# V projections of two head groups: 512 columns at once, weights in quarters of 256 rows

## Chip, cores and metric

The kernel runs on one core of a Trainium2 chip. The metric is the device time of one execution in microseconds (us). A core has TensorE (matmuls), VectorE, ScalarE, GpSimd and SyncE; the profile calls them PE, DVE, ACT, POOL and SP, and PEld is TensorE's weight load. Each engine runs its instructions in the order in which they were written out, and waits at semaphores for the others. Matmuls write to PSUM; GpSimd works on SBUF only.

## What is computed

Two layers of a trunk with 512 tokens and a width of 1024. In each, the normalised input `h` (512 x 1024) goes through one input projection, whose columns belong to three groups of heads: a (differential attention), b (stick-breaking), c (forgetting). Each group has q, k, v and gate columns, 512 of each:

```
h = rms_norm(x, g_pre)
p = h @ w_in
qa, ka, va, ga, qs, ks, vs, gs, qf, kf, vf, gf, ff = split(p)
ya = merge(diff_attention(rope(qa), rope(ka), va)) * silu(ga)
yb = merge(stick_breaking_attention(qs, ks, vs)) * silu(gs)
yc = merge(forgetting_attention(qf, kf, vf, cumsum(log_sigmoid(ff)))) * silu(gf)
x = x + rms_norm(concat([ya, yb, yc]) @ w_out, g_post)
```

All of it is in float32.

## The kernel before

A float32 product is made of three matmuls in the fp32r format. Each operand is kept as a rounded high part and the low rest, and `mm3` (L191) adds high x high, high x low and low x high in PSUM: L192, L193 and L194. The normalised input lies in SBUF, transposed, as two such parts (`hT`, 8 chunks of 128 rows by 512 tokens).

A weight unit has 256 columns of `w_in` and comes in two halves of 512 rows. `load_to` fetches a half into one of three `raw` buffers (SP's queue, L167). `split_to` makes the two parts of it in one of four `whl` buffers: ScalarE copies the high part in one instruction (L176, 128x1024), GpSimd subtracts it to get the low part in four pieces of 128x256 (L182). `load_to(st_split[0] + 3)` after each split asks for the raw tile three halves on.

Two forms of projection use the units. `proj_T` (q, k, gates) has the weights as the stationary operand and `hT` as the moving one, 512 columns wide, 24 matmuls for 128 output columns. `proj_N` (V) has a 128-token block of `hT` stationary and the weights moving, 256 columns wide: 24 matmuls for 128 tokens by 256 columns. ScalarE copies the result to the `v` tile (L649).

The order is written out by hand. `do(cost, fn)` puts a piece of projection on a planned time line (`now`, in planned ns) and moves it on by `cost`; `at(t, fn)` puts a side step at a planned time. In the end all steps are sorted by time and written out, so that the plan sets each engine's order, not its times. `use(k, t)` notes when half k is first needed, and its split is written out `lead` ns ahead of that.

For every layer the groups are projected in the order a, c, b: first V (8 blocks of `proj_N`, first unit's four token blocks, then the second's), then q, k, q, k (8 `proj_T`). While a group is projected, the attention of the group before it is run as side steps: `step_a` during c's projection, `step_c` during b's, `step_b` during the gates'. A score tile (L339) goes to VectorE, which adds the mask and takes the minimum (L364); then come exponentials on ScalarE (L373), transposes (L347) and the product with V.

After a projection of q or k, `qk_done` lets ScalarE copy the high part (L319) and VectorE make the low one (L324); for group a, VectorE's rope comes first (L303 to L307):

```
d = 2000 if roped else 0
return (rope_stages(st, scale) if roped else []) + [(d, hi), (d + 796, lo)]
```

Those numbers are plan times after the projection's end. The attention steps of a begin at 3518 after the start of c's stretch, those of c at 3191 after the start of b's.

Of the kernel before, what the change touches and what calls it, by code (L numbers as in the profile page):

```python
# [10 lines left out]
F32 = mybir.dt.float32  # L11
F32R = mybir.dt.float32r
BF16 = mybir.dt.bfloat16
AF = mybir.ActivationFunctionType
# [3 lines left out]
S = 512  # L18
DEPTH = 2
KC = D // 128  # L20
NT = S // 128
# [39 lines left out]
def hybrid_kernel(ctx, tc, x, w_in, forget_bias, diff_lambda, diff_subln, w_out, pre_norm, post_norm, consts, out):  # L61
    nc = tc.nc
# [5 lines left out]
    whl_p = P("whl", 4)  # L68
# [11 lines left out]
    pj_p = P("pj", 3, space=PS)  # L80
# [51 lines left out]
    now = [0.0]  # L132

    def do(cost, fn):
        main.append((now[0], 1, len(main), fn))
        now[0] += cost

    def at(t, fn):
        side.append((t, 0, len(side), fn))


    halves = []
# [3 lines left out]
    def add_in_unit(l, c0, extra=None):  # L146
        w = UW + (8 if extra is not None else 0)
        k0 = len(halves)
        for h in range(2):
            rows = w_in[l, h * 512:(h + 1) * 512]  # L150
            src = [(rows[:, c0:c0 + UW].rearrange("(k p) c -> p k c", p=128), 0, UW)]
            if extra is not None:
                src.append((rows[:, extra:extra + 8].rearrange("(k p) c -> p k c", p=128), UW, w))
            halves.append(dict(src=src, shape=[4, w], pool=whl_p, tag="whl", lead=9500 if h == 0 else 8000))
        return k0

    def add_out_unit(l, kc0, half, pool, tag):
        src = w_out[l, kc0 * 128:(kc0 + 2) * 128, half * S:(half + 1) * S].rearrange("(k p) c -> p k c", p=128)
        halves.append(dict(src=[(src, 0, S)], shape=[2, S], pool=pool, tag=tag, lead=10833))
        return len(halves) - 1  # L160
# [30 lines left out]
    def mm3(ps, lh, ll, rh, rl, first, last):  # L191
        nc.tensor.matmul(out=ps, lhsT=lh, rhs=rh, start=first, stop=False)  # L192
        nc.tensor.matmul(out=ps, lhsT=lh, rhs=rl, start=False, stop=False)  # L193
        nc.tensor.matmul(out=ps, lhsT=ll, rhs=rh, start=False, stop=last)  # L194
# [18 lines left out]
    def proj_N(k0, w, tt, hT, done):  # L213

        st = {}
        sl = slice(tt * 128, (tt + 1) * 128)

        def go(q):
            if q == 0:
                st["ps"] = pj_p.tile([128, w], F32, name="pj", tag="pj")  # L220
            for kc in range(4 * q, 4 * q + 4):
                u = halves[k0 + kc // 4]["hl"][:, :, kc % 4, :]
                h = hT()
                mm3(st["ps"], h[0][:, kc, sl], h[1][:, kc, sl], u[:, 0], u[:, 1], kc == 0, kc == KC - 1)

        for q in range(2):
            do(1290, lambda q=q: go(q))
        for t, fn in done(st):
            at(now[0] + t, fn)


    def pre_norm_stages(st, tt, hT):
# [307 lines left out]
    def decay_sum(lf, l):  # L540
        pt = pt_p.tile([8, S], F32, name="pt", tag="pt")
        for t in range(NT):
            nc.tensor.transpose(out=pt[:, t * 128:(t + 1) * 128], in_=lf[:, t * 8:(t + 1) * 8], identity=C["ident"])
        cum = cb_p.tile([8, S], F32, name="cum", tag="cb")
        nc.vector.tensor_tensor_scan(out=cum, data0=pt, data1=C["chunk"][0:8], initial=0.0, op0=ALU.add, op1=ALU.bypass)
        nc.sync.dma_start(out=cs[l], in_=cum)
# [6 lines left out]
    def steps(fn, c, t0, span, w=W_STEP):  # L553
        t = t0
        for p in range(4):
            for i in range(NT):
                fn(t, c, p, i)
                t += span / 16 * w[i]
# [3 lines left out]
    def use(k, t):  # L562
        uses.append((k, t))
# [43 lines left out]
    def plan_layer(l, L):  # L607
        hT = L["hT"]
# [8 lines left out]
        for g in ("a", "c", "b"):  # L617
            base = G[g]
            c = dict(pairs=[{} for _ in range(4)], lc=lc)
            st = {}  # L620
            c["v"] = lambda st=st: st["v"]
            c["o"] = lambda st=st: st["o"]
            c["cs"] = cs[l]
            t0 = now[0]
            at(t0, lambda st=st: st.update(v=v_p.tile([128, NT, 512], F32, name="v", tag="v")))
            if prev is not None:
                pst, pc, pg = prev
                at(t0, lambda pst=pst: pst.update(o=o_p.tile([128, 4, S], F32, name="o" + pg, tag="o")))
                steps(step_a if pg == "a" else step_c, pc, t0 + (3518 if pg == "a" else 3191), 50075 if pg == "a" else 46774)
            order = [(u, tt) for u in range(2) for tt in range(NT)]  # L630
            if g == "a":
                order = [(0, 0), (0, 1), (0, 2), (1, 0), (1, 1), (1, 2), (0, 3), (1, 3)]
            ks = []
            for u in range(2):
                ks.append(add_in_unit(l, base + 1024 + u * UW, 6144 if g == "a" and u == 0 else None))
            seen = set()
            for u, tt in order:
                ex = g == "a" and u == 0
                w = UW + (8 if ex else 0)
                if u not in seen:  # L640
                    seen.add(u)
                    use(ks[u], now[0])
                    use(ks[u] + 1, now[0] + 1300)
                    if g == "a" and u == 1:
                        halves[ks[u]]["lead"], halves[ks[u] + 1]["lead"] = 7500, 6500

                def done(pst, u=u, tt=tt, ex=ex, st=st, w=w):
                    def ev():
                        nc.scalar.activation(out=st["v"][:, tt, u * UW:(u + 1) * UW], in_=pst["ps"][:, 0:UW],  # L649
                                             func=AF.Copy)  # L650
                        if ex:
                            if "ff" not in ffd:
                                ffd["ff"] = lay.tile([128, 32], F32, name="ff", tag="ff")
                            nc.vector.tensor_copy(ffd["ff"][:, tt * 8:(tt + 1) * 8], pst["ps"][:, UW:w])
                    return [(0, ev)]
                proj_N(ks[u], w, tt, hT, done)
            if g == "a":
                at(now[0] + 2000, lambda: layer_consts(lcd, l))
                at(now[0] + 5000, lambda: ffd.update(lf=decay(ffd["ff"], lcd, l)))
                at(now[0] + 9000, lambda: decay_sum(ffd["lf"], l))  # L660
            sc = 0.125 if g == "b" else -0.125
            for u in range(2):
                for part in ("q", "k"):
                    k0 = add_in_unit(l, base + u * UW + (512 if part == "k" else 0))
                    use(k0, now[0])
                    use(k0 + 1, now[0] + 2600)
                    if g == "a" and u == 0 and part == "q":
                        for h in range(2):
                            halves[k0 + h].update(lead=2500, lo="both")
                    for cc in range(2):  # L670
                        keep = c["pairs"][2 * u + cc]
                        if part == "q":
                            proj_T(k0, cc, hT, lambda pst, keep=keep: qk_done(pst, g == "a", sc, keep, "q"))
                        else:
                            proj_T(k0, cc, hT, lambda pst, keep=keep: qk_done(pst, g == "a", 1.0, keep, "k"))
            prev = (st, c, g)
            ctxs[g] = (st, c)
# [27 lines left out]
        for g in ("b", "a", "c"):  # L705
            ost = ctxs[g][0]
            for u in range(2):
                k0 = add_in_unit(l, G[g] + 1536 + u * UW)
# [24 lines left out]
        order = [("a", 0), ("a", 2), ("c", 0), ("c", 2), ("b", 0), ("b", 2)]  # L733
        acc = {}
        for u, (g, j0) in enumerate(order):
            k = add_out_unit(l, row[g] + j0, 0, whl_p, "whl")
            use(k, now[0])
            for jj in range(2):
                for tt in range(NT) if (u, jj) == (5, 1) else (3, 0, 1, 2):
                    def go(u=u, g=g, j=j0 + jj, jj=jj, tt=tt, k=k):  # L740
                        if u == 0 and jj == 0:
                            acc[tt] = (pj_p if tt < 3 else s_p).tile([128, S], F32, name="acc",
                                                                    tag="pj" if tt < 3 else "s")
                        y, w = ys[g, j], halves[k]["hl"]
                        sl = slice(tt * 128, (tt + 1) * 128)
                        mm3(acc[tt], y[:, 0, sl], y[:, 1, sl], w[:, 0, jj], w[:, 1, jj],
                            u == 0 and jj == 0, u == 5 and jj == 1)
# [29 lines left out]
        for u, (g, j0) in enumerate(order):  # L777
            k = add_out_unit(l, row[g] + j0, 1, *((o_p, "o") if u < 3 else (v_p, "v") if u == 3 else (whl_p, "whl")))
# [3 lines left out]
        for tt in range(NT):  # L782
            sl = slice(tt * 128, (tt + 1) * 128)
            st = {}
# [56 lines left out]
    for l in range(DEPTH):  # L841
        L = plan_layer(l, L)
# [38 lines left out]
```

## Time and profile before

| | |
|---|---|
| time, median of 3 runs | 873.25 us (873.04 to 873.48) |
| time of the profiled execution | 873.66 us |
| its span, first to last instruction | 871.8 us |
| instructions | 13938 |
| TensorE busy | 854.9 us, 98% of the span |
| VectorE / ScalarE / GpSimd busy | 495.3 / 476.9 / 449.6 us |

The profile is one execution. A row of a timeline is a start, a length, the engine, the line in the kernel, the operation, output<-input with shapes, a count, and in brackets how long the engine sat idle before it and what ended the wait. Matmuls are pipelined, so that a matmul's length is longer than the distance to the next start; that distance, the pitch, is what one costs in a row of them.

### The profile page before, as it was taken

How to read it: one execution, taken by the hardware profiler on the slowest of the kernel's cores; microseconds unless marked ns; L12 is line 12 of the kernel's file. 1: busy time of each engine (PE TensorE's matmuls, PEld its weight loads, DVE VectorE, ACT ScalarE, POOL GpSimd, SP SyncE). 2: the span in 40 equal slices, each digit the busy share in tenths (PEclk: the TensorE clock that was granted, in tenths of full speed). 3: DMA queues.
4: the chain of work that ended last, by engine and by line, in shares of the span. 5: the costliest groups of instructions: out<-in, count | busy, mean ns of one | idle time of the engine just before them, and what ended most of it. 6: DMA issues, size and time to landing. Idle time of an engine off the chain costs nothing.

```text
span 871.8 us, 13938 instructions
## 1 busy us (share of the span) xinstructions
PE 854.9 (98%) x4892; PEld 721.4 (83%) x4892; DVE 495.3 (57%) x1143; ACT 476.9 (55%) x1064; POOL 449.6 (52%) x680
## 2 busy tenths in 40 slices
PE   7999999999999999999999999999999999999997
PEld 5988998898778778777898889888987787877885
DVE  5378656544565778623563875664445476774322
ACT  4344667766776556633334356676667756664310
POOL 4366554655444548770364664555554544688301
PEclk9999999999999999999999999999999999999999
DMA  7365323432524221237264452325335422122522
GB/s 233 89 164 138 96 73 98 117 102 76 154 67 116 75 72 49 73 107 257 78 177 114 123 145 74 99 72 146 97 81 137 106 66 72 49 78 92 164 101 97
DMA packets 73207, 94.27 MB, mean 108 GB/s; under 512 B 6433, under 2 KB 56225, under 8 KB 73138
## 3 DMA queue, kind: packets, MB, share of 16 engines
q1 hardware_dynamic: 70834, 89.19, 35.6%
q10 hardware_dynamic: 2304, 4.20, 1.5%
q8 instruction: 39, 0.64, 0.3%
q14 instruction: 30, 0.25, 0.1%
HBM read 76.56 MB, written 4.23 MB: 93 GB/s over the span
## 4 chain that ended last, share of the span: by engine, by line
PE 78%; DVE 10%; ACT 4%; POOL 3%; issue 2%; DMA 2%; DVEq 0%; POOLq 0%; ACTq 0%; SPq 0%
PE pj L192 18%; PE pj L194 18%; PE pj L193 17%; PE s L339 6%; PE pt L347 5%; PE ov L437 4%; POOL hl L182 2%; PE acc L192 2%; PE acc L193 2%; PE acc L194 2%; PE ov L399 2%; DVE ra L307 2%; DVE sh L306 2%; DVE sh L303 1%; DVE qd L324 1%
## 5 line engine op out<-in xcount | busy, mean ns | idle before, releaser
L182 POOL TENSOR_TENSOR hl<-raw,hl 128x256 fp32r<-128x256 f32 (+1 forms) x420 | 343.5, 850 | 237.1 <-ACT hl L176 213.0
L192 PE MATMUL pj<-hT,hl 128*128 128x512 f32 x576 | 236.6, 411 | 0.0
L194 PE MATMUL pj<-hT,hl 128*128 128x512 f32 x576 | 225.7, 392 | 0.0
L193 PE MATMUL pj<-hT,hl 128*128 128x512 f32 x576 | 225.3, 391 | 0.0
L176 ACT ACTIVATE hl<-raw 128x1024 fp32r<-128x1024 f32 (+1 forms) x120 | 126.3, 1058 | 35.4 <-DMA raw<-in_w_out_dram 18.9
L194 PEld LDWEIGHTS pj<-hT,hl 128*128 128x128 f32 x576 | 108.1, 188 | 24.3
L192 PEld LDWEIGHTS pj<-hT,hl 128*128 128x128 f32 x576 | 108.4, 188 | 20.0 <-issue 2.1
L193 PEld LDWEIGHTS pj<-hT,hl 128*128 128x128 f32 x576 | 108.7, 189 | 16.9
L192 PE MATMUL pj<-hl,hT 128*128 128x256 f32 (+1 forms) x384 | 112.2, 292 | 0.3 <-ACT hT L257 0.2
L194 PE MATMUL pj<-hl,hT 128*128 128x256 f32 (+1 forms) x384 | 109.5, 285 | 0.5 <-DVE hT L258 0.5
L193 PE MATMUL pj<-hl,hT 128*128 128x256 f32 (+1 forms) x384 | 109.3, 285 | 0.5 <-POOL hl L182 0.5
L373 ACT ACTIVATE p<-p,mn 128x128 f32<-128x128 f32 (+3 forms) x128 | 71.1, 556 | 33.6 <-DVE mn L364 31.7
L506 DVE TENSOR_TENSOR_SCAN kp<-kp,c_masks 128x128 f32<-128x128 f32 (+3 forms) x64 | 67.2, 1051 | 18.3 <-ACT kp L499 17.8
L192 PEld LDWEIGHTS pj<-hl,hT 128*128 128x128 f32 x384 | 73.7, 192 | 1.3 <-ACT hT L257 1.0
L193 PEld LDWEIGHTS pj<-hl,hT 128*128 128x128 f32 x384 | 73.8, 192 | 1.2 <-POOL hl L182 0.7
L194 PEld LDWEIGHTS pj<-hl,hT 128*128 128x128 f32 x384 | 73.5, 191 | 1.2 <-DVE hT L258 1.2
L339 PE MATMUL s<-kd,qd 128*128 128x128 f32 (+1 forms) x192 | 62.6, 330 | 2.9 <-DVE mn L364 2.9
L350 ACT ACTIVATE pT<-pt 128x128 f32<-128x128 f32 (+3 forms) x96 | 41.2, 443 | 37.5 <-PE pt L347 37.2
L339 PE MATMUL s<-kd,qs 128*128 128x128 f32 (+1 forms) x192 | 61.2, 323 | 0.0
L511 DVE TENSOR_TENSOR sg<-sg,kp 128x127 f32<-128x127 f32 (+3 forms) x64 | 46.1, 721 | 5.5
L185 DVE TENSOR_TENSOR hl<-raw,hl 128x1024 fp32r<-128x1024 f32 (+2 forms) x18 | 21.0, 1175 | 44.8 <-ACT hl L176 44.7
L466 ACT ACTIVATE p<-p,rc 128x128 f32<-128x128 f32 (+3 forms) x64 | 35.0, 556 | 20.2 <-DVE rc L464 20.2
(142 smaller groups left out, 1453.0 us busy)
## 6 DMA issues: line engine op xcount, KB each, us to landing
raw<-in_w_in_dram SPq DMA_DIRECT2D x96, 512.0 KB, 3.7
qs<-qd SPq DMA_DIRECT2D x48, 256.0 KB, 4.5
raw<-in_w_out_dram SPq DMA_DIRECT2D x24, 512.0 KB, 3.6
cb<-cs ACTq DMA_DIRECT2D x16, 256.0 KB, 3.3
xl<-in_x_dram SPq DMA_DIRECT2D x4, 512.0 KB, 4.9
xt<-in_x_dram SPq DMA_DIRECT2D x8, 256.0 KB, 6.1
xs<-xt SPq DMA_DIRECT2D x8, 256.0 KB, 2.0
xt<-xs SPq DMA_DIRECT2D x8, 256.0 KB, 3.9
```

The lines of the kernel that those rows point to most:

```text
L176: nc.scalar.activation(out=hl[:, 0], in_=raw, func=AF.Copy)
L182: nc.gpsimd.tensor_tensor(out=hl[:, 1, k, c:e], in0=raw[:, k, c:e], in1=hl[:, 0, k, c:e].bitcast(F32), op=ALU.subtract)
L192: nc.tensor.matmul(out=ps, lhsT=lh, rhs=rh, start=first, stop=False)
L193: nc.tensor.matmul(out=ps, lhsT=lh, rhs=rl, start=False, stop=False)
L194: nc.tensor.matmul(out=ps, lhsT=ll, rhs=rh, start=False, stop=last)
L339: nc.tensor.matmul(out=s[:, 0:n], lhsT=pr[q][:, m, i * 128:n], rhs=pr["k"][:, m, 0:n], start=(j == 0), stop=(j == 1))
L347: nc.tensor.transpose(out=pt[:, j * 128:(j + 1) * 128], in_=p[:, j * 128:(j + 1) * 128], identity=C["ident"])
L350: nc.scalar.activation(out=t, in_=src, func=AF.Copy)
L373: nc.scalar.activation(out=p[:, 0:n], in_=p[:, 0:n], func=AF.Exp, bias=st["mn", m], scale=-1.0, accum_out=su)
L466: nc.scalar.activation(out=p[:, 0:n], in_=p[:, 0:n], func=AF.Copy, scale=r)
L506: nc.vector.tensor_tensor_scan(out=rv, data0=rv, data1=C["first"][:, S - n:S][:, ::-1], initial=0.0, op0=ALU.mult, op1=ALU.max)
L511: nc.vector.tensor_tensor(out=sg[:, 0:n - 1], in0=sg[:, 0:n - 1], in1=kp[:, 1:n], op=ALU.mult)
```

## The change

Groups b and c no longer use `add_in_unit` and `proj_N` for V, but `add_v_unit` and `proj_V`: four quarters of 256 rows by 512 columns, each in one `whl` buffer, and four token blocks of 24 matmuls with 512 moving columns. Each quarter is still split by one copy on ScalarE and four pieces on GpSimd, two for each 128 rows. The quarters' leads are 9500, 8000, 5100 and 3800, and the two halves of the first q unit behind them get leads of 3800 and 5100. Group a is as it was.

```diff
+    def add_v_unit(l, c0):
+
+        k0 = len(halves)
+        for h in range(4):
+            src = w_in[l, h * 256:(h + 1) * 256, c0:c0 + S].rearrange("(k p) c -> p k c", p=128)
+            halves.append(dict(src=[(src, 0, S)], shape=[2, S], pool=whl_p, tag="whl", lead=(9500, 8000, 5100, 3800)[h]))
+        return k0
...
+    def proj_V(k0, tt, hT, done):
+
+        st = {}
+        sl = slice(tt * 128, (tt + 1) * 128)
+
+        def go(q):
+            if q == 0:
+                st["ps"] = pj_p.tile([128, S], F32, name="pj", tag="pj")
+            h = hT()
+            for kc in range(2 * q, 2 * q + 2):
+                u = halves[k0 + q]["hl"][:, :, kc % 2]
+                mm3(st["ps"], h[0][:, kc, sl], h[1][:, kc, sl], u[:, 0], u[:, 1], kc == 0, kc == KC - 1)
+
+        for q in range(4):
+            do(1296, lambda q=q: go(q))
+        at(now[0], lambda: done(st["ps"]))
...
-            for u in range(2):
+            if g != "a":
+                order = []
+                kv = add_v_unit(l, base + 1024)
+                for h in range(4):
+                    use(kv + h, now[0] + 1296 * h)
+                for tt in range(NT):
+                    proj_V(kv, tt, hT, lambda ps, st=st, tt=tt: nc.scalar.activation(out=st["v"][:, tt], in_=ps, func=AF.Copy))
+            for u in range(2 if g == "a" else 0):
                 ks.append(add_in_unit(l, base + 1024 + u * UW, 6144 if g == "a" and u == 0 else None))
...
+                    if g != "a" and u == 0 and part == "q":
+                        for h in range(2):
+                            halves[k0 + h]["lead"] = (3800, 5100)[h]
```

## Rows read from the trace of the kernel before

**Rows 1.** The page, part 1: busy us, share of the span, count

```profile
PE 854.9 (98%) x4892; PEld 721.4 (83%) x4892; DVE 495.3 (57%) x1143; ACT 476.9 (55%) x1064; POOL 449.6 (52%) x680
```

**Rows 2.** Waits of TensorE: total us, times, longest; the largest group

```profile
PE s L339 <- DVE mn L364: 2.9, 4, 1.1
```

**Rows 3.** Stretches of the V projections, layer 0: length, busy us per engine

```profile
84.35:115.90 31.55, 30.37 (x249) 29.79 (x248) 17.98 (x57) 20.34 (x53) 16.23 (x24) 1.00 0.33 91
178.18:208.76 30.58, 30.58 (x254) 29.89 (x253) 12.39 (x61) 20.69 (x53) 17.63 (x31) 1.00 0.28 83
```

**Rows 4.** Timeline, TensorE: first and last of 36 matmuls of 256 columns

```profile
25.02 0.28 PE L192 MATMUL pj<-hl,hT 128*128 128x256 f32 x1
...
29.21 0.28 PE L194 MATMUL pj<-hl,hT 128*128 128x256 f32 x1
```

**Rows 5.** Timeline, TensorE: first and last of 149 matmuls of 512 columns

```profile
50.55 0.39 PE L193 MATMUL pj<-hT,hl 128*128 128x512 f32 x1
...
84.13 0.39 PE L194 MATMUL pj<-hT,hl 128*128 128x512 f32 x1
```

**Rows 6.** Timeline, ScalarE, start of group c, layer 0

```profile
85.18 1.28 ACT L319 ACTIVATE kd<-ra 64x512 fp32r<-64x512 f32 x2 [3.24 <-DVE ra L307]
86.49 1.06 ACT L176 ACTIVATE hl<-raw 128x1024 fp32r<-128x1024 f32 x1
90.78 1.28 ACT L319 ACTIVATE kd<-ra 64x512 fp32r<-64x512 f32 x2 [3.23 <-DVE ra L307]
```

**Rows 7.** Timeline, VectorE, the same stretch

```profile
88.55 1.05 DVE L306 SCALAR_TENSOR_TENSOR sh<-sh,rope 128x512 f32<-128x512 f32 x1
89.64 1.11 DVE L307 TENSOR_TENSOR ra<-ra,sh 128x512 f32<-128x512 f32 x1
91.45 1.40 DVE L324 SCALAR_TENSOR_TENSOR kd<-ra,kd 64x512 fp32r<-64x512 f32 x2 [0.70 <-ACT kd L319]
```

**Rows 8.** Timeline, GpSimd: four split pieces merged, then the second and third singly

```profile
87.62 3.72 POOL L182 TENSOR_TENSOR hl<-raw,hl 128x256 fp32r<-128x256 f32 x4 [1.89 <-ACT hl L176]
...
88.32 0.74 POOL L182 TENSOR_TENSOR hl<-raw,hl 128x256 fp32r<-128x256 f32 x1
...
89.01 1.19 POOL L182 TENSOR_TENSOR hl<-raw,hl 128x256 fp32r<-128x256 f32 x1
```

**Rows 9.** Timeline, TensorE: a score and the matmul behind it; the longest wait

```profile
88.67 0.22 PE L339 MATMUL s<-kd,qd 128*128 128x128 f32 x1
...
88.84 0.33 PE L192 MATMUL pj<-hl,hT 128*128 128x256 f32 x1
...
93.24 0.39 PE L339 MATMUL s<-kd,qd 128*128 128x256 f32 x1 [1.09 <-DVE mn L364]
```

**Rows 10.** Timeline, start of the kernel: two split pieces, a matmul released by them

```profile
11.06 2.44 POOL L182 TENSOR_TENSOR hl<-raw,hl 128x264 fp32r<-128x264 f32 x2 [1.31 <-ACT hl L176]
...
13.55 0.39 PE L193 MATMUL pj<-hl,hT 128*128 128x264 f32 x1 [0.51 <-POOL hl L182]
```

**Rows 11.** Timeline, ScalarE and GpSimd, start of group b, layer 0

```profile
178.38 1.20 ACT L319 ACTIVATE kd<-pj 64x512 fp32r<-64x512 f32 x2 [1.86 <-PE pj L194]
179.60 1.06 ACT L176 ACTIVATE hl<-raw 128x1024 fp32r<-128x1024 f32 x1
...
180.74 2.83 POOL L182 TENSOR_TENSOR hl<-raw,hl 128x256 fp32r<-128x256 f32 x4 [4.66 <-ACT hl L176]
```

**Rows 12.** Timeline, TensorE and ScalarE, end of c's stretch, layer 0

```profile
108.55 0.22 PE L339 MATMUL s<-kd,qd 128*128 128x128 f32 x1
...
115.90 0.48 PE L192 MATMUL pj<-hT,hl 128*128 128x512 f32 x1
...
110.28 0.60 ACT L350 ACTIVATE wT<-pt 128x512 f32<-128x512 f32 x1 [1.01 <-PE pt L347]
```

**Rows 13.** Timeline, TensorE: two of the first projection matmuls, 264 columns

```profile
10.54 0.42 PE L193 MATMUL pj<-hl,hT 128*128 128x264 f32 x1
10.76 0.42 PE L194 MATMUL pj<-hl,hT 128*128 128x264 f32 x1
```

## The prediction

> **What bounds the kernel now.** I read the busy shares first: TensorE is busy for 98% of the span, no other engine for more than 57% [rows 1]. Next, TensorE's own waits: the longest group is 2.9 us in four waits, for a minimum that VectorE takes off the scores [rows 2]. So TensorE runs in order and almost without a gap; its instruction time is the kernel's time, and whatever it newly has to wait for is added to it.
>
> Then the four stretches that the change touches, the V projection of groups c and b in both layers: layer 0's two stand in [rows 3], and layer 1 repeats them. Each holds 192 projection matmuls and the attention steps of the group before. TensorE is busy all through b's; c's stretch has 1.2 us of idle time, nearly all of it one wait [rows 3, 9].
>
> Last, the timelines of ScalarE, VectorE and GpSimd around 84.35 us, where c's V projection begins. Before it lie a's roped q and k projections, and there the other engines do not keep up: ScalarE's copies (L319) of the second last and the last k projection start at 85.18 and 90.78, each as soon as VectorE's rope is done, though TensorE has ended the last of them by 84.35; the weight splits stand in line between [rows 6].
>
> **The change part by part.**
>
> *Matmuls.* In each stretch 192 matmuls of 256 columns become 96 of 512. Pitch at 256: from 25.02 to 29.21 in 35 steps, 0.1197 us [rows 4]. Pitch at 512: from 50.55 to 84.13 in 148 steps, 0.227 us [rows 5]. A planned piece of 12 narrow matmuls (1.436 us) becomes one of 6 wide ones (1.362): 0.074 us less, over 16 pieces 1.19 us per stretch, 4.75 us in all. This is the gain on offer, as TensorE has no other slack.
>
> The rows say that a matmul costs its columns at 2.4 GHz and 12 to 14 ns more [rows 4, 5]. The Trainium skill, "TensorE: Matmul & The Clock Gate", section "Back-to-back issue gap", puts the fixed part of a warm matmul at 2.5 ns; by that a pair saves 2.6 ns and not 12, a stretch about 0.25 us, and the sum below would be about 3.2 us higher. This trace differs from it, and the measured pitches are used.
>
> *Evictions.* Eight ScalarE copies of 256 columns become four of 512. They are off TensorE's path, which has three PSUM buffers; counted as nothing. If that cover failed, a late copy would hold the third next tile, over 10 us on.
>
> *Loads and splits.* Bytes, GpSimd pieces (16 of 128x256 per stretch) and ScalarE copies (four) stay. The raw tiles are asked for three splits ahead on SP, so their landing costs nothing; if that cover went, quarter 3 would come later still.
>
> *When the weights are needed.* Here the cost lies. Before, the first row block needs only two halves (columns 0 to 255), and the other two 10.3 us of plan later. Now the first row block walks through all four quarters in 5.5 us. Quarters 2 and 3 can't be split early: they take the buffers of the last k unit, so they are written out at plan times -2508 and +88 against the stretch's start, both behind the second last k copy (plan -3184) and ahead of the last (+2000). In ScalarE's line that is the slot of the split at 86.49 to 87.55 [rows 6]; quarter 3 follows at 87.55 to 88.6, since ScalarE now idles there until 90.78 and its raw tile was asked for three splits before. GpSimd takes quarter 2 as it takes that split now: 87.62 to 91.34, the second of the four pieces ending at 89.05 [rows 8]. The first two pieces take a turn of 0.70 each; the last two, beside VectorE's L306 and L307, whose operands are all in SBUF, 1.16 [rows 7, 8].
>
> TensorE in group c, layer 0: pieces 0 and 1 end at 84.35 + 12 x 0.227 = 87.07. Row 4's second matmul streams the low part of all 512 columns, so it waits for two pieces: 89.05 and a release of 0.05 (13.50 to 13.55 at the kernel's start, where a matmul waits for one row's piece only [rows 10]) gives 89.10. Third matmul 89.33, row 5's first 89.55, its second with the fourth piece at 91.39, end 91.84. The first score takes 0.17 [rows 9]: 92.01. Quarter 3 starts on GpSimd at 91.34 while VectorE runs L324 twice on SBUF operands (from 91.45 [rows 7]). How GpSimd fares beside L324 no row shows; bounds are 0.70 and 1.16 a piece. I take 1.16 for the two beside L324 and 0.70 after: 93.66 and 95.06. Row 6's second matmul runs at 93.71, row 7's first at 94.16, its second at 95.11, end 95.56. With the second score (0.17) and the next piece (1.36) TensorE is at the scores of the next step at 97.10. Now it gets there at 93.24, after its wait of 1.09 [rows 9], which the later start swallows. Loss 3.86; all pieces at 0.70 give 2.94, all at 1.16 give 4.77. The other 11 pieces give back 0.82. Group c: **+3.04** per layer (2.1 to 3.95).
>
> Behind quarter 3 on ScalarE stand the last k copy, which waits for VectorE anyway, and the first exponentials, which depend on scores that now come late too; on GpSimd nothing of step a is due.
>
> Group b follows unroped projections. ScalarE idles from 176.5 to 178.38 [rows 11], so quarter 2 is copied there and split by about 180.4, before its need at 178.18 + 2.72 = 180.9. Quarter 3 takes the place of the split at 179.60, its pieces ending 181.45 to 183.57 [rows 11]; row 7 needs the last at about 183.39, so 0.24 is lost. Group b: -1.19 + 0.24 = **-0.95** per layer. From below -1.19 (no wait); from above, quarter 2 at 1.16 a piece pushes quarter 3's end to 185.04, a wait of 1.7, +0.5.
>
> *The q unit behind.* It takes the quarters' buffers, with leads cut to 3800 and 5100. Quarter 0 is free at 108.55 in today's times, the first q matmul runs at 115.90 [rows 12], 7.3 us on. ScalarE first copies a transposed tile (ends 110.88) and a square, so the split runs from about 111.2 to 112.2, and GpSimd's first piece is there by 113.0. Group b is alike. Nothing, with 2.5 us in hand; if gone, each microsecond costs one, four times.
>
> Sum: 2 x 3.04 - 2 x 0.95 = +4.2 us. On the profiled execution (873.66 us; span 871.8 and 1.86 around it) 877.9; that execution lies 0.41 above the median of 873.25, so I say **877.4** for the median. Bounds: 2 x (2.1 - 1.19) = +1.8, 875.1; 2 x (3.95 + 0.5) = +8.9, 882.2.
>
> **Rivals.** A run within 0.2% (1.75 us) of 873.25 counts as no change; measurement tells no less.
>
> *The weights come in time* (faster). Quarters 2 and 3 are ready in group c before 87.3 and 88.7. Then c's stretches keep 0.82 (the first five pieces' gain goes into the wait at 93.24) and b's 0.95: -3.5 us, 869.7. It decides once row 7's last piece ends before 92.9, since the loss then falls below 0.82 + 0.95. For it: the loads are early. Against: eight pieces from 87.62 at the best rate of 0.70 end at 93.2, and ScalarE can't begin before the k copy ends at 86.46 [rows 6]. Chance 0.10.
>
> *Half the wait*, some overlap that I miss (release by piece order, VectorE done earlier): +1 us, 874.3. Chance 0.05.
>
> *Wide matmuls save nothing here*, at 0.239 per 512 columns: the gains of 2 x 0.82 + 2 x 1.19 go, 881.4. Against it: 148 steps at 0.227. The skill's issue gap, cited above, leans this way. Chance 0.04.
>
> *The clock falls in the new waits.* In group c TensorE would be idle for some 5.6 of 8.5 us, the longest gap 1.6. At the start of the kernel matmuls of 264 columns run at a pitch of 0.22, the 1.2 GHz level, later at 0.12 [rows 4, 13]; that lasts 2.9 us. If it returned for as long, 7 wide matmuls lose some 0.2 each, 1.4 us, and with what falls into the waits' gaps up to 2 per layer: 881. Against it: the granted clock is 1.00 over both stretches of [rows 3], the gap of 1.09 at 93.24 among them [rows 9]. The same page of the Trainium skill, in "Why this matters for your kernels", warns that a long idle gap between bursts drops the array to half rate; no gap in this trace is long enough to show it. Chance 0.07.
>
> *The q unit comes late as well*, by a microsecond at four places, because ScalarE lags behind its exponentials: 881.4. Chance 0.06.
>
> **Numbers.** The forecast has 0.68. Faster holds 0.10, no change 0.06 (the half wait and a little of the forecast), slower 0.84. The range runs from 874.2 to 881.8: it leaves out the faster case and the tail above. The likeliest case's own range is 875.1 to 882.2.
>
> **What would show it.** In the profile after: TensorE waits for GpSimd's split (L182) shortly after the start of c's stretches, three of 1.3 to 1.6 us and a shorter one, over 5 us in a layer; the wait for the minimum at the next step's scores gone; quarters 2 and 3 copied by ScalarE back to back between two k copies; b's stretches about a microsecond shorter; pitch 0.227 in the V projection. I would be wrong if the k copies stood behind the splits in ScalarE's line, if GpSimd gave the pieces in another order, or if TensorE's waits moved to the q projections.

## The result, and the profile after

The changed kernel takes 879.67 us (four runs, 877.83 to 881.18); before it was 873.25 (873.30 with a fourth run). The ratio is 1.0072, with a 95% interval of [1.0051, 1.0094]: 6.4 us slower. The forecast was 877.4 in a range of 874.2 to 881.8: the side is right and the time is inside, but the loss is half as large again as forecast. The four runs differ more than those of before, and go with their mean granted clock: 0.995 in the shortest, 0.991 in the longest, which is the profiled one (span 879.3).

The page after, busy shares and the clock by fortieths of the span:

```profile
PE 858.4 (98%) x4508; PEld 703.9 (80%) x4508; DVE 499.6 (57%) x1143; ACT 475.1 (54%) x1048; POOL 451.2 (51%) x680
...
PEclk9999899999999999999999989999999999999999
```

TensorE issues 384 matmuls fewer than in [rows 1] and yet is busy for 3.5 us longer. The two digits of 8 lie in fortieths that hold a part of c's stretch, one in layer 0 and one in layer 1 (87.9 to 109.9 and 505.6 to 527.6 us).

Two of TensorE's wait groups after (us in all, times, longest), to set against [rows 2], whose group is no longer there (in the new file `mm3` is L200 to L202, the split L184 and L190, the scores L364, the k copies L344 and L349, the minimum L389):

```profile
PE pj L201 <- POOL hl L190: 6.7, 10, 1.3
...
PE pj L200 <- ACT hl L184: 0.8, 2, 0.4
```

The four stretches after: length, busy us of PE, PEld, DVE, ACT and POOL, granted clock, DMA share, GB/s:

```profile
84.44:121.08 36.64, 33.16 (x154) 26.43 (x152) 19.28 (x57) 19.37 (x48) 14.98 (x22) 0.91 0.18 49
183.54:213.41 29.87, 29.87 (x157) 24.71 (x156) 12.65 (x61) 19.01 (x48) 13.37 (x25) 1.00 0.20 63
515.38:551.62 36.24, 33.15 (x154) 26.30 (x152) 19.28 (x57) 19.37 (x48) 14.98 (x22) 0.91 0.18 51
614.08:643.95 29.87, 29.87 (x158) 24.72 (x156) 12.52 (x61) 19.05 (x48) 13.39 (x25) 1.00 0.23 66
```

Against [rows 3] (31.55 and 30.58, the same in both layers) c's stretches are 5.09 and 4.69 us longer and b's 0.71 shorter each. The rest of the span: the q and k projections behind c's stretch +0.18 and +0.19, what lies behind b's -0.54 and -0.76, and +0.09 ahead of c in layer 0. These nine make +7.5, by which the spans differ.

Where c loses it, layer 0. TensorE:

```profile
87.70 0.51 PE L200 MATMUL pj<-hl,hT 128*128 128x512 f32 x1 [0.38 <-ACT hl L184]
...
89.20 0.50 PE L201 MATMUL pj<-hl,hT 128*128 128x512 f32 x1 [0.99 <-POOL hl L190]
...
91.46 0.50 PE L201 MATMUL pj<-hl,hT 128*128 128x512 f32 x1 [1.30 <-POOL hl L190]
...
93.29 0.80 PE L201 MATMUL pj<-hl,hT 128*128 128x512 f32 x1 [0.64 <-POOL hl L190]
...
95.12 0.80 PE L201 MATMUL pj<-hl,hT 128*128 128x512 f32 x1 [0.18 <-POOL hl L190]
...
99.13 0.41 PE L364 MATMUL s<-kd,qd 128*128 128x256 f32 x1
```

ScalarE, GpSimd and VectorE in the same place:

```profile
85.28 1.28 ACT L344 ACTIVATE kd<-ra 64x512 fp32r<-64x512 f32 x2 [3.25 <-DVE ra L332]
86.59 2.01 ACT L184 ACTIVATE hl<-raw 128x1024 fp32r<-128x1024 f32 x2
90.86 1.28 ACT L344 ACTIVATE kd<-ra 64x512 fp32r<-64x512 f32 x2 [2.27 <-DVE ra L332]
...
87.72 7.34 POOL L190 TENSOR_TENSOR hl<-raw,hl 128x256 fp32r<-128x256 f32 x8 [1.88 <-ACT hl L184]
...
91.52 2.26 DVE L349 SCALAR_TENSOR_TENSOR kd<-ra,kd 64x512 fp32r<-64x512 f32 x2 [0.69 <-ACT kd L344]
```

TensorE takes each weight part as it is made. Both quarters are copied in one go between the two k copies of [rows 6], and the eight pieces end at 95.06. The last wait ends at 95.12; then TensorE waits for nothing until the scores at 99.13, and takes 4.01 us for eight wide matmuls and a score, where the prediction's sum has 1.99. The windows around it tell why (columns as above; the last three numbers are the clock, DMA and GB/s):

```profile
90.00:92.00 2.00, 0.70 (x3) 0.48 (x3) 1.30 (x2) 1.11 (x2) 2.00 (x3) 1.00 0.00 0
92.00:94.00 2.00, 1.36 (x6) 0.92 (x5) 1.94 (x3) 1.43 (x2) 2.00 (x3) 0.73 0.66 175
94.00:96.00 2.00, 1.82 (x5) 1.00 (x4) 0.11 (x2) 0.50 (x2) 1.06 (x2) 0.50 0.25 87
...
98.00:100.00 2.00, 2.00 (x9) 1.71 (x8) 0.21 (x1) 0.07 (x1) 0.00 (x0) 0.56 0.11 36
100.00:104.00 4.00, 4.00 (x21) 3.37 (x20) 2.92 (x15) 1.59 (x6) 0.00 (x0) 1.00 0.00 0
```

The granted clock is 0.50, the 1.2 GHz level, from about 92.9 to 99.8 (worked out from the mixed windows: 0.73 at 92 to 94, 0.56 at 98 to 100). The wide matmuls of 97.42 to 98.70 are 0.43 apart, those from 99.88 on 0.23. The bracketed waits are shorter than TensorE's loss, since a matmul's length runs on over its pitch: by the pitch the wait before 89.20 is 89.20 - 87.70 - 0.23 = 1.27, not 0.99.

Layer 1 has the same first three waits (0.38, 0.99 and 1.30), but there the clock falls before the fourth, at about 523.0, while TensorE is at work:

```profile
522.40 0.50 PE L201 MATMUL pj<-hl,hT 128*128 128x512 f32 x1 [1.30 <-POOL hl L190]
...
524.24 0.80 PE L201 MATMUL pj<-hl,hT 128*128 128x512 f32 x1 [0.24 <-POOL hl L190]
```

It is back at about 529.8. So the clock is low for 6.8 us in both layers.

### The profile page after: what moved, and what is told of

Same layout as the page of the kernel before. It is cut to its first block, busy times and chain, and to the rows that moved or that the text cites. A ratio compares the mean times of both kernels' runs of the same rounds, so it can differ in the third digit from the quotient of the medians.

```text
span 879.3 us, 13146 instructions
## 1 busy us (share of the span) xinstructions
PE 858.4 (98%) x4508; PEld 703.9 (80%) x4508; DVE 499.6 (57%) x1143; ACT 475.1 (54%) x1048; POOL 451.2 (51%) x680
## 4 chain that ended last, share of the span: by engine, by line
PE 82%; POOL 10%; issue 5%; DMA 1%; DVE 1%; ACT 1%; DVEq 0%; POOLq 0%; SPq 0%
PE pj L200 19%; PE pj L202 18%; PE pj L201 18%; POOL hl L190 9%; PE s L364 7%; PE pt L372 5%; PE ov L462 4%; PE acc L200 2%; PE acc L201 2%; PE acc L202 2%; PE ov L424 2%; PE pt L279 1%; DMA gain<-in_post_norm_dram 1%; DMA xl<-in_x_dram 0%; PE pt L440 0%
## 5 line engine op out<-in xcount | busy, mean ns | idle before, releaser
L190 POOL TENSOR_TENSOR hl<-raw,hl 128x256 fp32r<-128x256 f32 (+1 forms) x420 | 345.2, 855 | 203.7 <-ACT hl L184 179.3
L200 PE MATMUL pj<-hT,hl 128*128 128x512 f32 x576 | 236.6, 411 | 0.0
L202 PE MATMUL pj<-hT,hl 128*128 128x512 f32 x576 | 225.8, 392 | 0.0
L184 ACT ACTIVATE hl<-raw 128x1024 fp32r<-128x1024 f32 (+1 forms) x120 | 126.2, 1058 | 35.1 <-DMA raw<-in_w_out_dram 18.9
L202 PEld LDWEIGHTS pj<-hT,hl 128*128 128x128 f32 x576 | 108.1, 188 | 24.3
L200 PEld LDWEIGHTS pj<-hT,hl 128*128 128x128 f32 x576 | 108.4, 188 | 19.8 <-issue 2.1
L201 PE MATMUL pj<-hl,hT 128*128 128x512 f32 (+2 forms) x256 | 90.1, 352 | 6.7 <-POOL hl L190 6.7
L200 PE MATMUL pj<-hl,hT 128*128 128x512 f32 (+2 forms) x256 | 91.9, 359 | 1.0 <-ACT hl L184 0.8
L202 PE MATMUL pj<-hl,hT 128*128 128x512 f32 (+2 forms) x256 | 88.9, 347 | 0.5 <-DVE hT L283 0.5
L375 ACT ACTIVATE pT<-pt 128x128 f32<-128x128 f32 (+3 forms) x96 | 41.3, 443 | 42.1 <-PE pt L372 41.9
L364 PE MATMUL s<-kd,qd 128*128 128x128 f32 (+1 forms) x192 | 62.1, 328 | 0.0
L201 PEld LDWEIGHTS pj<-hl,hT 128*128 128x128 f32 x256 | 49.7, 194 | 15.0 <-POOL hl L190 11.6
L364 PE MATMUL s<-kd,qs 128*128 128x128 f32 (+1 forms) x192 | 61.6, 325 | 0.0
L200 PEld LDWEIGHTS pj<-hl,hT 128*128 128x128 f32 x256 | 49.8, 195 | 6.9 <-ACT hl L184 1.6
L202 PEld LDWEIGHTS pj<-hl,hT 128*128 128x128 f32 x256 | 49.7, 194 | 6.3 <-DVE hT L283 1.2
L481 POOL TENSOR_TENSOR cm<-cb,c_causal 128x128 f32<-128x128 f32 x64 | 28.1, 462 | 38.2 <-DMA cb<-cs 20.9
```

What stands on the lines that cost most here:

```text
L184: nc.scalar.activation(out=hl[:, 0], in_=raw, func=AF.Copy)
L190: nc.gpsimd.tensor_tensor(out=hl[:, 1, k, c:e], in0=raw[:, k, c:e], in1=hl[:, 0, k, c:e].bitcast(F32), op=ALU.subtract)
L364: nc.tensor.matmul(out=s[:, 0:n], lhsT=pr[q][:, m, i * 128:n], rhs=pr["k"][:, m, 0:n], start=(j == 0), stop=(j == 1))
L375: nc.scalar.activation(out=t, in_=src, func=AF.Copy)
```

## The experiments

Two theories stood at the start. *Late weights*: c's loss is the wait for quarters 2 and 3, which can't be split earlier in ScalarE's and GpSimd's lines. *Clock*: half of it or more is the slow clock behind the waits. A third, that wide matmuls save nothing, was a rival of the prediction. Behind each time stand its ratio to the kernel before and the ratio's 95% interval. Line numbers differ a little from version to version; the names of the tiles tell which step a row is.

**b alone wide.** Group c is as before: the three places that treat b and c alike now treat only b so.

```diff
-            if g != "a":
+            if g == "b":
...
-            for u in range(2 if g == "a" else 0):
+            for u in range(0 if g == "b" else 2):
```

> Only group b takes 512 columns at once, group c stays as before. Theory (the loss lies in group c's start, where the split of quarters 3 and 4 comes late): c's stretches are back at 31.55 us, b's stay at 29.87, so about 1.4 us faster than before and up to 1 us more from the later stages, 871.3 us (870.7 to 872.2). Rival (the wide V projection costs wherever it is used, by its four buffers or by the q unit behind it): b alone brings half of the loss, about 876.5.

870.32 us, 0.9964 [0.9951, 0.9976]: 2.9 to 3.1 us faster than before, a little more than was expected, and the lowest median of all versions. Stretch b and the waits:

```profile
177.88:207.76 29.88, 29.88 (x158) 24.72 (x157) 12.66 (x61) 19.03 (x48) 13.35 (x25) 1.00 0.21 66
```

```profile
PE s L364 <- DVE mn L389: 2.1, 2, 1.1
```

c's stretches are 31.55 and 31.51 again. b's are 0.70 shorter, the clock is 1.00 in these stretches, and the rest (1.0 and 0.8 us) is won behind b's stretch, where two of the four waits of [rows 2] are gone; 0.6 of the 1.0 is a shorter wait between the layers (see the filled kernel below). So all of the loss is c's.

**c walked by quarters.** The first three token blocks go through quarters 0 and 1, then the three through quarter 2, then 3; the fourth block follows whole. The same matmuls, loads and splits, but quarter 2 is needed some 5.4 us later.

```diff
+    BY_QUARTER = [(0, (0, 1)), (1, (0, 1)), (2, (0, 1)), (0, (2,)), (1, (2,)), (2, (2,)),
+                  (0, (3,)), (1, (3,)), (2, (3,)), (3, (0, 1, 2, 3))]
+    V_ORDER = {"c": BY_QUARTER, "b": IN_TURN}
...
-                for tt in range(NT):
-                    proj_V(kv, tt, hT, ...)
+                for tt, qs in V_ORDER[g]:
+                    proj_V(kv, tt, qs, hT, ...)
```

> As the changed kernel, but in group c three token blocks go through the first two quarters before any goes through the third and fourth, in three PSUM tiles; every split stays where it is. Theory: the third quarter is first needed 8 us after the stretch's start and the fourth 12 us after it, when both are long split; no wait for GpSimd's split, clock at full rate, c's stretches about 30.8 us, 869.9 us in all (869.2 to 870.8). Rival (the loss is not the order in which the weights are needed): still above 876.

873.3 us (11 runs, 871.37 to 874.31), 0.9995 [0.9986, 1.0003]. The theory's 869.9 was missed. The waits for the split in c are gone, and with them 6.4 us. But nothing is won on the kernel before: TensorE now comes early to the scores of the next step (L367 here) and waits there for VectorE's minimum (L392). The scores in layer 0 and 1, and VectorE's low part of k (L352) ahead of the first:

```profile
93.72 0.38 PE L367 MATMUL s<-kd,qd 128*128 128x256 f32 x1 [2.33 <-DVE mn L392]
...
519.67 0.58 PE L367 MATMUL s<-kd,qd 128*128 128x256 f32 x1 [2.94 <-DVE mn L392]
...
91.07 2.27 DVE L352 SCALAR_TENSOR_TENSOR kd<-ra,kd 64x512 fp32r<-64x512 f32 x2 [0.70 <-ACT kd L347]
```

```profile
83.97:115.50 31.53, 29.20 (x154) 24.55 (x152) 19.22 (x57) 19.37 (x48) 14.99 (x22) 1.00 0.20 56
...
509.28:544.10 34.82, 31.88 (x153) 26.60 (x152) 19.82 (x58) 19.36 (x48) 15.61 (x22) 0.90 0.21 56
```

VectorE's low part of k, 1.40 us in [rows 7], takes 2.27 beside GpSimd's split, which now lies there. The scores come 9.75 us after the stretch's start, where before it was 8.89; the rest of the stretch is 0.88 shorter. So layer 0's stretch is as long as before. Layer 1's is the same program text and 3.3 us longer; its granted clock is 0.90. In the profiled run those 3.3 us take all that b's stretches and what lies behind them give back. The 11 runs go with their mean granted clock in the same way: 871.37 us at 0.999, 874.31 at 0.995.

**The waits filled.** 22 matmuls of 512 columns are put into the waits of c's first block; they write to a spare PSUM tile that nobody reads. Late weights stay late, but TensorE isn't idle.

```diff
+    FILL = {(4, 0): 2, (4, 1): 5, (5, 1): 6, (6, 1): 6, (7, 1): 3}
...
+            for _ in range(FILL.get((kc, j), 0)):
+                nc.tensor.matmul(out=junk, lhsT=h[0][:, 0, 0:128], rhs=h[0][:, 0], start=True, stop=True)
```

> As the changed kernel, with 22 matmuls of 512 columns on data that is there, into an unused PSUM tile, put into the first token block of group c in front of the matmuls that wait; nothing reads their result. Theory (part of the loss is the clock that falls in these waits): the waits for the splits are as long, but TensorE is never idle in them; granted clock 1.00 in c's stretches, which last about 34.6 us, and 876.4 us in all (875.8 to 877.2). Rival (the half rate has another cause than the waits): clock 0.90 in c's stretches and 879 to 881.

```profile
84.24:118.78 34.54, 34.54 (x175) 28.43 (x174) 19.30 (x57) 19.38 (x48) 15.01 (x22) 1.00 0.18 51
...
515.64:550.24 34.60, 34.60 (x175) 28.43 (x174) 19.35 (x57) 19.37 (x48) 15.04 (x22) 1.00 0.19 54
```

In the stretches this is the cleanest reading: clock 1.00 and 2.99 and 3.05 us above before, where 3.04 was forecast. So in the profiled run of the change late weights cost 3.0 per layer and the clock 2.1 and 1.6, less than the half that the second theory had. The total came out otherwise than expected, 879.99 us, 1.0076 [1.0064, 1.0088]: between the layers TensorE waited 2.11 us for VectorE, which waited for the load of the post-norm gains (0.98 before, 0.39 with b alone wide), and the clock fell behind that wait, for about 3.4 us:

```profile
409.59 0.50 PE L200 MATMUL pj<-hl,yv 128*128 128x512 f32 x1 [2.11 <-DVE y L806]
```

```profile
410.00:412.00 2.00, 2.00 (x7) 1.51 (x6) 1.33 (x3) 0.00 (x0) 0.00 (x0) 0.52 1.06 405
```

**The same with 18 matmuls.**

> As c_fill with 18 instead of 22 matmuls in the waits. Theory: clock 1.00 and 34.6 us in c's stretches as there; in all 876.5 us, unless TensorE waits for the gains' load between the layers as long as in c_fill (2.1 us, and a stretch at half rate behind it), then 880. Rival (c_fill's extra matmuls cost about what the clock gave back): 879 without such a wait.

877.36 us (877.12 to 877.71), 1.0049 [1.0033, 1.0064]. c's stretches are 34.58 both with clock 1.00, the gains' wait is 1.68, and no clock falls behind it:

```profile
84.10:118.68 34.58, 34.09 (x172) 27.69 (x170) 19.32 (x57) 19.38 (x48) 15.04 (x22) 1.00 0.19 52
```

TensorE is idle for 0.5 us of it, and the stretch is no shorter than with 22 matmuls: the filling itself adds nothing that can be seen. This is the changed kernel without the clock's fall, at the time that the prediction gave it.

**Quarter 2 split earlier.** One lead of c (`halves[kv + 2]["lead"] = 6392`) puts its split ahead of the second last k copy.

> As the changed kernel, but in group c the third quarter's split is written out 1.3 us of plan earlier, ahead of the second last k copy in ScalarE's line. Theory: GpSimd begins it at about 85.8 instead of 87.7 and ends the fourth quarter's last piece at about 93.2 instead of 95.1; TensorE's loss at the next step's scores falls from 3.9 to about 2.0 us per layer. 873.5 us if the clock then stays up, 876 if it falls as well. Rival (GpSimd's order is not what TensorE waits for): 879 to 881.

874.85 us (12 runs, 872.58 to 878.90), 1.0013 [1.0000, 1.0026]. GpSimd now ends the last piece at 92.87, 1.9 us earlier against the stretch's start, and the four waits are 0.18, 0.87, 0.63 and 0.74; the one for ScalarE is gone. The last:

```profile
92.92 0.80 PE L201 MATMUL pj<-hl,hT 128*128 128x512 f32 x1 [0.74 <-POOL hl L190]
```

The lateness moves as the split does. In the profiled run the clock still falls (0.90 and 0.95 over the two stretches, 35.2 and 34.2 long). The runs spread over 6 us and part by their mean granted clock: five with 0.998 or more take 872.58 to 873.44 us, seven with 0.996 or less 874.70 to 878.90, against the 873.5 and 876 that were expected without and with a fall.

**Quarter order, narrow matmuls.** As c by quarters, but each wide matmul is two of 256 columns, in c and in b.

> As c_by_quarter, with quarters, buffers, splits, copies and order as they are, but each matmul of 512 columns as two of 256 in both groups. Theory (b's stretch is shorter through the pitch alone): b's stretches grow from 29.88 to 30.6, their length before; c's by up to 0.6, less what the wait for VectorE takes back; 875 us (874 to 876.5). Rival (b's gain comes from fewer copies or from the later need of the weights): b's stretches stay at 29.9, 873.5.

874.72 us, 1.0018 [1.0009, 1.0027], as expected. b's stretches:

```profile
180.20:210.80 30.60, 30.60 (x254) 29.92 (x253) 12.67 (x61) 19.11 (x48) 13.57 (x26) 1.00 0.20 63
```

30.6 narrow against 29.88 wide, with the same quarters and splits: width alone is worth 0.7 us in b's stretch, and quarters alone cost nothing there. What width is worth in c these two kernels don't tell: TensorE waits for VectorE either way (2.00 and 1.99 us here), and the clock falls in both of c's stretches here (33.64 us each) and in one of them with c by quarters.

**Attention of a later.** The scores near the start of c's stretch wait for VectorE, so the steps of a were begun 2592 planned ns later, first with their end kept (16 steps over 47483 planned ns in place of 50075), then with their spacing kept, the tail running into b's stretch.

```diff
-  steps(..., t0 + (3518 if pg == "a" else 3191), 50075 if pg == "a" else 46774)
+  steps(..., t0 + (6110 if pg == "a" else 3191), 47483 if pg == "a" else 46774)
```

> As c_by_quarter, and the attention steps of group a begin 2592 ns of plan (two pieces) later in c's stretch, ending at the same plan time as before. Theory (with the weights in time, c's start is bound by VectorE, whose rope and low part keep the first minimum until 93.4, and TensorE waits there because the order puts the next scores in front of projection that it could do): TensorE reaches those scores at about 94 and does not wait; c's stretches 29.4 us, clock 1.00, 866.5 us in all (865.5 to 868.5). Rival (the steps are only pushed together and wait further on): 871 or more.

> As b_only (group c in 256 columns), with the same later start of group a's attention steps. Theory: the wait of 1.09 us before the second step's scores goes in both layers, 1.2 us each, c's stretches 30.3 us, 867.9 us in all (867.2 to 869). Rival (as for c_by_quarter_late): 870 or more. The distance to c_by_quarter_late is what 512 columns are worth in group c once nothing is waited for: by the pitch of 0.230 there 0.9 us per layer, by that of 0.227 1.2.

Both expectations failed: 879.87 us (1.0078 [1.0066, 1.0091]) with c by quarters, 882.61 (1.0110 [1.0097, 1.0124]) with b alone wide. c's stretch gets short (27.86 in the first), but the denser steps behind it wait for VectorE, the transposes (L375) for the combined weights (L417):

```profile
PE pt L375 <- DVE p L417: 6.1, 4, 1.7
```

c's stretch and the q and k projections together take 97.8 us, against 94.0 in c by quarters.

> As c_by_quarter_late, but the attention steps of group a keep their spacing (50075) and all begin 2592 ns of plan later. Theory (c_by_quarter_late lost because its steps were pushed together, so that a step's chain through VectorE and ScalarE was not done when its transposes came up): no waits for the combined weights (L417 there) in the q and k projections, none at c's start; stretch and q and k projections of c together 91.5 us (94.0 in c_by_quarter, 97.8 in c_by_quarter_late), 868 us in all (867 to 870). Rival (any later start puts those chains beside the copies of the q and k projections, where they come late): waits for L417 as in c_by_quarter_late, 875 or more.

> As b_only, with the same shift at unchanged spacing. Theory: stretch and q and k projections of group c together 92.6 us (93.8 in b_only), 868 us in all (867 to 869.5). Rival: as for c_by_quarter_shift, 874 or more.

With the spacing kept the same sums are 92.52 and 92.76 us, where 91.5 and 92.6 were expected: here the move does win. But b's stretch now gets ScalarE late, behind the tail of a's steps, and waits for its own split (32.28 us against 29.88):

```profile
176.67:208.95 32.28, 30.63 (x158) 24.92 (x157) 12.98 (x62) 19.44 (x49) 13.12 (x25) 1.00 0.16 50
```

Both times missed the 868 that was expected of each: 873.69 us (1.0004 [0.9994, 1.0013]) and 874.46 (1.0013 [1.0004, 1.0021]).

**The same with b by quarters**, first with c by quarters (`V_ORDER["b"] = BY_QUARTER`), then with c narrow as before.

> As c_by_quarter_shift, with group b's V projection in the order by quarters too. In c_by_quarter_shift group c keeps its gain (stretch with q and k projections 92.5 us against 93.8 before), but the later end of its attention steps delays ScalarE's copy of group b's fourth quarter, and b's stretch waits for the split (32.3 us against 29.9). Theory (the wait hangs on the order in which b needs its quarters): b's stretches back at about 29.9 us, 868.5 us in all (867.5 to 870.5). Rival (in b the time goes to VectorE's and ScalarE's chains, as in c): b's stretches above 31.5, 872 or more.

> As b_only_shift, with group b's V projection in the order by quarters. Theory: the waits for the split in b's stretch go, 29.9 us each; with 92.8 us for c's stretch and its q and k projections 869.2 us in all (868 to 870.5), about a microsecond better than b_only. Rival as for cb_by_quarter_shift: 872 or more.

870.59 us, 0.9974 [0.9966, 0.9983], and 871.98, 0.9994 [0.9983, 1.0004], where 868.5 and 869.2 were expected. The split waits of b's stretch go, its length is 31.28, not 29.9, and a wait for the minimum takes their place:

```profile
PE s L367 <- DVE mn L392: 1.8, 2, 0.9
```

With both groups wide this is as fast as b alone wide (the two intervals overlap), not faster.

## Why the prediction was right, and where it was short

*Where the cost lies*: right. Quarters 2 and 3 sit between the two k copies in ScalarE's line, the pieces come at GpSimd's turn, and TensorE takes them one by one. The last piece was put at 95.06 and ended at 95.06; the second matmuls of the four rows at 89.10, 91.39, 93.71 and 95.11 ran at 89.20, 91.46, 93.29 and 95.12. The third is 0.4 off because the two slow pieces of quarter 3 were its second and third (1.17 and 1.18 us, the others 0.73), not its first two. The sign "over 5 us in a layer" did not come: by the brackets TensorE's waits for the split are 3.1 us in layer 0 and 2.7 in layer 1, as a matmul's length counts into its pitch and the last ones ran at the low clock. Taking the loss away by order (c by quarters), moving it by a lead (quarter 2 earlier) and doing without it (b alone wide) all bear this out.

*Group c, +3.04 per layer*: right without the clock (34.54 to 34.60 against 31.55, four stretches), though partly by luck: with 18 matmuls filled in, 4.02 is lost up to the next step's scores (97.01 - 84.10 against 93.24 - 84.35; forecast 3.86) and 0.99 given back behind them (forecast 0.82). It is short of the changed kernel's 5.09 and 4.69. What was mis-sized is the rival *the clock falls in the new waits*: its price, up to 2 us per layer, was right (2.1 and 1.6), its chance of 0.07 was too low, as all four runs show a mean granted clock of 0.995 or less, against 0.998 in the profile of before. The argument against it was one gap of 1.09 us that left the clock at 1.00 [rows 9]. Behind waits of 0.38, 0.99 and 1.30 it fell, in layer 0 within the next one, of 0.64, in layer 1 before it. The Trainium skill, "TensorE: Matmul & The Clock Gate", section "Why this matters for your kernels", warns of a long idle gap between bursts; here no single long gap stood before the fall, so that this section's warning, taken alone, would have foretold none. The measurement decides. The duration was taken as 2.9 us from the kernel's start and was 6.8; the price stayed at about 2 because the first 2.2 us of it in layer 0, and 3.1 in layer 1, lie ahead of the end of the last wait, where TensorE was waiting for the pieces anyway.

*Group b, -0.95 per layer*: the stretch gave -0.71. There was hardly a wait; the pitch was the error. It was taken from a projection with nothing between the matmuls [rows 5], 0.227; in b's stretch, beside the attention steps, it is longer, as in these five steps of 0.232:

```profile
191.73 0.40 PE L200 MATMUL pj<-hl,hT 128*128 128x512 f32 x1
...
192.89 0.39 PE L202 MATMUL pj<-hl,hT 128*128 128x512 f32 x1
```

Over the whole stretch 85 of the 96 steps take 0.230 on average, and the other eleven about 0.31. From start to next start the 96 wide matmuls add up to 22.98 us, and the 192 narrow ones before to 23.69: 0.71 less. Why the pitch is longer here no run settles. (A slip of the prediction beside it: the 2.6 ns that it works out for a pair is 2.5; nothing hangs on it.)

*Evictions, loads, the q unit: nothing*. Right as far as the trace can say: no wait for either stands in the waits of after. The q and k projections behind c's stretch are 0.18 and 0.19 longer. Not foreseen was a gain of 0.5 to 0.8 behind b's stretch, where a wait for the minimum (two of [rows 2]'s four) is gone.

*The sum*: with these sizes and without the clock, 2 x 3.03 - 2 x 0.71 + 2 x 0.18 - 1.30 = +3.7 against +4.2 forecast, and +4.1 from 873.25 to the 877.36 of the kernel with 18 matmuls filled in, whose gains' wait is 0.7 longer than before. That 877.36 meets the forecast of 877.4 is partly luck: b gave less, what lies behind b gave 1.3 that the sum did not have, and the gains' wait took half of that back. The clock adds 2.1 + 1.6 = 3.7 in the profiled run, which is the longest of the four; the median has 2.3 us more than the filled kernel. That the measured time is inside the range is partly luck as well: the room above 877.4 was made for slower pieces and a wait in b, and it was the clock that took it up.

*The rival that the weights come in time* (869.7): its price was wrong too. It credited c with 0.82 and b with 0.95. With the weights in time c gains nothing (31.53, or 3.3 more where the clock falls), since VectorE's chain from rope to the minimum sets the next scores, and GpSimd's split slows that very chain. The "0.82" (0.88 measured) is lost ahead of those scores, which come 0.86 later, behind a wait of 2.33 us.

Open: what decides whether the clock falls, as one layer of c by quarters keeps it and the other not, and runs of one kernel differ; why the gains' load ends later in some versions (waits of 0.4 to 2.1 us between the layers), which moves totals by more than a microsecond and is why the stretches were compared; that wait was not taken away in any run.

## What to carry to other kernels

When a tile's shape changes at the same bytes, ask when each part of the weights is first needed and where its preparation stands in the line of the engine that makes it: here 384 matmuls fewer lost to eight split pieces per layer that came too late for the new order. Price the wait that is behind the one you remove as well, and take an instruction's pitch from the stretch in which it will run. A bundle of short waits can cost more than their sum: here the clock fell behind them. The same change in one group alone kept the gain without the waits.

## What the runs showed of the hardware

The clock fell to 0.50 (1.2 GHz) behind several short waits, none above 1.30 us, and stayed there for 6.8 us. Behind a single longer wait it was not the same each time: in c by quarters it held after 2.33 us in layer 0 and fell within the 2.94 us of layer 1, for 6.8 us; in the filled kernel it fell behind 2.11 us, for 3.4. It held after the 1.68 us with 18 matmuls. With the waits filled by matmuls it held in all four stretches of c.

VectorE's pair of instructions with both inputs in SBUF took 2.26 us beside GpSimd's pieces and 1.40 alone, and GpSimd's pieces are longer there too: 1.17 and 1.18 us beside the pair, 0.73 just before and after. The Trainium skill, "SBUF — State Buffer", section "Who interferes with whom", says that a VectorE instruction with two SBUF inputs contends with a GpSimd one that reads SBUF; the trace agrees, and here both engines pay. This cost showed only once TensorE no longer came late to the scores.
